# The sample rows' back products of a scan group join the insert of the last chunk's output

## The chip, the cores and the metric

The kernel runs on one core of one Trainium2 chip. The metric is the device time of one execution in microseconds. Before the change the median of three runs was 1186.1 us (1184.93 to 1188.74).

The core has five engines that run their own instruction queues in order and wait for each other by semaphores: TensorE (PE in the profile, with its weight loads as PEld), VectorE (DVE), ScalarE (ACT), GpSimd (POOL) and SyncE (SP), which here only issues DMA transfers.

## The reference, cut to what matters

One layer of a decoder: a wide input projection feeds a Mamba-2 scan (SSD) and an RG-LRU branch; both are projected, gated, merged and normed, and a gated ConvFFN follows. 512 prompt rows and 32 sample rows (8 sequences of 4 tokens, each with a state of its own) go through it together. The change touches the scan alone, which is computed for four groups of eight heads:

```python
    cb = jnp.einsum('bclgn,bcsgn->bclsg', Cm, Bm)
    y_diag = jnp.einsum('bclsg,bclsgh,bcsghp->bclghp', cb, decay, xdt)
    decay_to_end = jnp.exp(a_cs[:, :, -1:] - a_cs)
    states = jnp.einsum('bclgn,bclgh,bclghp->bcghpn', Bm, decay_to_end, xdt)
...
    y_off = jnp.einsum('bclgn,bcghpn,bclgh->bclghp', Cm, h_prev, jnp.exp(a_cs))
    y = (y_diag + y_off).reshape(b, L, SSD_HEADS, P)
...
    y = y + d_skip[:, None] * xs
    y = y.reshape(b, L, D_SSD) * jax.nn.silu(z)
```

The prompt is four chunks of 128 tokens; a sample sequence is one chunk of four tokens that starts from its stored state.

## The kernel before

**Slots.** Activations lie with channels on partitions and the 544 rows along the free axis. Every weight block of 128 output channels is one slot of the list `order`. A slot runs two half slots, 256 and then 288 columns, of 24 matmuls each (`mm3`, line 194: eight steps of the contraction, three products for a split of both operands into two fp32r parts); the weights are split into `wh` and `wl` (lines 199 and 200) two slots ahead and loaded four slots ahead into three buffers. Behind every half slot the kernel calls `hook()`.

**Inserts.** What isn't a weight slot is put between half slots. `spread(fn, slots)` fills the deque `side` with tasks and `set_rate` divides their number by the hooks of the slots (less one); each `hook()` adds this rate to a sum and runs a task for every whole number reached. So the number of tasks sets where each of them falls. The scan of group 0 is spread over ten slots (20 hooks, `p0`), those of groups 1 and 2 over fourteen (28 hooks, with the finished group's gates ahead of them), that of group 3 over twelve (24 hooks).

**A group's tasks.** `mixed_tasks(g)` (line 660) makes them of four prompt units a, b, c, d (`unit`) and one sample unit (`sample_unit`). For a prompt chunk: `s0` loads rows into E (line 441; two buffers for four chunks) and `eb`, `ep` masks E on POOL (L453) and takes exponentials on ScalarE (L456), `s1` transposes on TensorE (L465 to L467), `e1` and `e2` make `xdt` (L472, VectorE), `xde` (L474, POOL) and E times the products (L481), `st` makes the state product (L485), `pd` the products with E (L494), `py` the products with the carried state (L507), `up`, `yd` and `yo` bring these together (L511 on POOL; L513, L514, L501, L520 on VectorE).

For the sample rows, `s2(q)` for q = 0 to 3 (the tasks q0 to q3) treats two sequences each: a state product (L606), the old state times its decay on POOL (L607), and their sum on VectorE (L608), which a store then writes out. q0 and q2 also take the products of four old states with C (L600), and q2 those within the chunk (L631, TensorE) and makes from both the tile y (`joined`: L637, then four L640, all VectorE). The last task, `s4` (called f), multiplies y back into channel layout: four products (L646; eight passes in the profile, since fp32 takes two) and four VectorE operations that update the sample columns of x (L649). f needs y complete.

**Order.** Tasks put instructions into the program in this order; the library's scheduler then orders each engine's queue, and may bring instructions ahead of others that have to wait by its reckoning. Thus the next group's `s0` and `ep` (E loads on SP, L453 on POOL, L456 on ScalarE) stand ahead of much of a group's last tasks. SP issues all loads and stores, and waits in its queue wherever a buffer isn't free.

Of the kernel before, what the change touches and what calls it, by code (L numbers as in the profile page):

```python
# [78 lines left out]
def kernel(ctx: ExitStack, tc: tile.TileContext, xT, W, wdt, wab, par, con, tri,  # L79
# [574 lines left out]
    def both(*fns):  # L654
        def run():
            for f in fns:
                f()
        return run

    def mixed_tasks(g):  # L660

        a, b, c, d = (unit(g, i) for i in range(NCH))
        p0, p1, pe, q0, q1, q2, q3, f = sample_unit(g)

        def steps(*names):
            return both(*[u[n] for u, n in names])

        def first(u, v):
            return steps((u, "s1"), (v, "s1"), (u, "e1"), (v, "e1"), (u, "e2"), (v, "e2"))
        return [both(a["s0"], b["s0"], p0), steps((a, "ep"), (b, "ep")), both(p1, first(a, b)), pe,  # L670
                steps((a, "st"), (b, "st"), (a, "pd"), (b, "pd"), (a, "yd"), (b, "yd"), (c, "s0"), (d, "s0")),
                both(b["py"], q0, b["up"], b["yo"]), both(q1, c["ep"]), d["ep"], first(c, d), lambda: None,
                steps((c, "st"), (d, "st"), (c, "py"), (c, "pd"), (d, "pd"), (c, "up"), (c, "yd"), (d, "yd"), (c, "yo")),
                q2, both(d["py"], q3, d["up"], d["yo"]), f]


    yh, yl = {}, {}
# [586 lines left out]
    def p0():  # L1264
        xbc_cb(1)
        xbc_xs(1)
        zs(0)
    spread(lambda: mixed_tasks(0), p0)

    def p12(g):  # L1270
# [6 lines left out]
    def gated(g):  # L1277
        t = mixed_tasks(g)
        gt = gate_tasks(g - 1)
        return ([both(*gt[:2]), both(*gt[2:], t[0])] if g < 3 else [both(*gt), t[0]]) + t[1:]  # L1280
# [270 lines left out]
```

## Time and profile before

| | |
|---|---|
| median of three runs | 1186.1 us |
| profiled execution | 1185.91 us |
| its span | 1183.6 us |
| PE busy | 1171.3 us, 99% of the span |
| DVE, ACT, POOL busy | 751.9, 550.3 and 248.5 us |
| mean granted TensorE clock | 0.996 |
| weight matmuls' share of the chain that ended last (L194) | 88% |
| scan of the four groups | between about 65 and 434 us |

The busy time of an engine is the sum of its instructions' time without overlaps. The chain that ended last is followed back from the last instruction to what released each step; where one engine never waits, it is that engine's own instructions in order. In the rows of the chain and of the timeline the first column is the start from the beginning of the span, the second the duration; both are in us, and a number behind x counts instructions. "[0.87 <-ACT w L696]" means that the engine sat idle for 0.87 us before it, and what ended this.

### The profile page before, as it was taken

The page shows a single profiled execution, that of the slowest core. Times are in us where ns is not written, and L with a number is a line of the kernel's source. Part 1 is how long each engine was busy: PE and PEld are TensorE (multiplying, and loading weights), DVE is VectorE, ACT ScalarE, POOL GpSimd, SP SyncE. Part 2 cuts the span into 40 slices and gives each one's busy share as a digit, 9 for nine tenths or more (in the row PEclk, how much of TensorE's full clock was granted, in tenths as well). Part 3 has the DMA queues.
Part 4 walks back from the last instruction along what each step waited for, and adds up shares of the span by engine and source line. Part 5 has one row for each costly group of instructions (what it writes and reads, how often), then busy time and mean ns, then how long its engine had stood idle before and what let it go on. Part 6 is the DMA issues. An engine that isn't in the chain of part 4 may idle for free.

```text
span 1183.6 us, 22963 instructions
## 1 busy us (share of the span) xinstructions
PE 1171.3 (99%) x9390; PEld 1142.3 (97%) x9390; DVE 751.9 (64%) x1244; ACT 550.3 (46%) x1048; POOL 248.5 (21%) x341
## 2 busy tenths in 40 slices
PE   9999999999999999999999999999999999999997
PEld 7998999999999999999999999999999999999996
DVE  6888767786798777956733448774434444344456
ACT  6573654454454437568332326654313342134423
POOL 1453434343342322100100015100000010001023
PEclk9999999999999999999999999999999999999998
DMA  7436525434452621332322454442222232222312
GB/s 261 133 118 208 173 84 187 145 116 153 155 170 85 196 99 58 109 103 66 102 86 89 127 163 129 125 140 90 90 90 90 90 89 90 87 84 86 94 53 76
DMA packets 53465, 138.70 MB, mean 117 GB/s; under 512 B 5872, under 2 KB 16240, under 8 KB 53360
## 3 DMA queue, kind: packets, MB, share of 16 engines
q1 hardware_dynamic: 53360, 137.24, 36.4%
q8 instruction: 73, 1.20, 0.4%
q14 instruction: 32, 0.26, 0.1%
HBM read 124.72 MB, written 12.50 MB: 116 GB/s over the span
## 4 chain that ended last, share of the span: by engine, by line
PE 96%; DMA 1%; DVE 1%; POOL 1%; SPq 0%; issue 0%; ACT 0%; ACTq 0%; POOLq 0%
PE ps L194 88%; PE ps L494 1%; PE ps L485 1%; PE ps L507 1%; PE ps L606 1%; DMA x<-xT 1%; PE ps L600 1%; PE ps L465 1%; DMA E<-scr_a 0%; DMA wr<-W 0%; PE ps L646 0%; PE ps L467 0%; PE ps L937 0%; PE ps L944 0%; POOL h L607 0%
## 5 line engine op out<-in xcount | busy, mean ns | idle before, releaser
L194 PE MATMUL ps<-n,wh 128*128 128x256 f32 (+1 forms) x5472 | 1034.0, 288 | 1.2 <-ACT wh L199 0.8
L194 PEld LDWEIGHTS ps<-n,wh 128*128 128x128 f32 x5472 | 858.9, 188 | 7.1 <-ACT wh L199 2.0
L194 PE MATMUL ps<-n,wl 128*128 128x256 f32 (+1 forms) x2736 | 786.8, 288 | 0.1
L194 PEld LDWEIGHTS ps<-n,wl 128*128 128x128 f32 x2736 | 514.8, 188 | 0.3 <-DVE wl L200 0.3
L200 DVE TENSOR_TENSOR wl<-wr,wh 128x1024 fp32r<-128x1024 f32 (+1 forms) x183 | 226.1, 1235 | 193.1 <-ACT wh L199 192.7
L199 ACT ACTIVATE wh<-wr 128x1024 fp32r<-128x1024 f32 (+1 forms) x183 | 191.9, 1049 | 333.5 <-PE ps L194 295.6
L358 POOL COPY cffn_t<-w 128x18 f32<-128x18 f32 x24 | 18.8, 783 | 344.4 <-ACT w L1032 344.4
L362 DVE SCALAR_TENSOR_TENSOR w<-w,half_t,w 128x568 f32<-128x568 f32 x72 | 61.9, 863 | 2.4 <-ACT w L360 1.4
L362 DVE SCALAR_TENSOR_TENSOR w<-w,par_t,w 128x560 f32<-128x560 f32 (+1 forms) x72 | 59.3, 823 | 4.0 <-ACT w L360 1.0
L456 ACT ACTIVATE E<-E,nac_t 128x128 f32<-128x128 f32 x128 | 39.2, 390 | 7.1 <-POOL E L453 7.1
L199 ACT ACTIVATE n<-n 128x544 fp32r<-128x544 f32 (+2 forms) x56 | 32.2, 584 | 17.5 <-DVE n L833 10.7
L1064 DVE TENSOR_TENSOR n<-n,ps 128x256 f32<-128x256 f32 (+1 forms) x40 | 17.5, 438 | 34.6 <-PE ps L194 20.6
L607 POOL TENSOR_TENSOR h<-h,cds_t 128x512 f32<-128x512 f32 x32 | 35.7, 1147 | 6.1 <-PE ps L600 6.0
L713 POOL TENSOR_TENSOR ss<-ss,x 128x544 f32<-128x544 f32 x15 | 25.4, 1691 | 49.9 <-ACT x L712 49.4
L200 DVE TENSOR_TENSOR n<-n,n 128x544 fp32r<-128x544 f32 (+2 forms) x56 | 35.6, 641 | 0.3
L1039 ACT ACTIVATE n<-w 128x512 f32<-128x512 f32 (+1 forms) x48 | 18.2, 424 | 35.7 <-DVE w L362 35.7
L407 ACT ACTIVATE w<-w 128x568 f32<-128x568 f32 x24 | 16.3, 678 | 35.8 <-DVE w L362 35.8
L1098 DVE TENSOR_TENSOR n<-n,ps 128x256 f32<-128x256 f32 (+1 forms) x24 | 10.4, 432 | 35.5 <-PE ps L194 35.4
L1030 ACT ACTIVATE w<-ps 128x256 f32<-128x256 f32 x48 | 18.0, 375 | 31.0 <-PE ps L194 31.0
L474 POOL TENSOR_TENSOR xde<-xdt,dte_t 128x512 f32<-128x512 f32 x16 | 22.4, 1412 | 45.6 <-DVE xdt L472 45.6
L194 PE MATMUL ps<-n,n 128*128 128x256 f32 (+1 forms) x240 | 31.1, 290 | 0.0
L194 PEld LDWEIGHTS ps<-n,n 128*128 128x128 f32 x240 | 30.4, 188 | 0.1
(239 smaller groups left out, 1035.5 us busy)
## 6 DMA issues: line engine op xcount, KB each, us to landing
wr<-W SPq DMA_DIRECT2D x184, 512.0 KB, 3.5
E<-scr_a SPq DMA_DIRECT2D x16, 512.0 KB, 5.1
h<-h0T SPq DMA_DIRECT2D x32, 256.0 KB, 5.0
o_sst<-h SPq DMA_DIRECT2D x32, 256.0 KB, 2.3
eb<-scr_e SPq DMA_DIRECT2D x24, 128.0 KB, 4.8
n<-xT SPq DMA_DIRECT2D x8, 272.0 KB, 3.9
yT<-w SPq DMA_DIRECT2D x4, 288.0 KB, 2.3
x<-xT SPq DMA_DIRECT2D x4, 272.0 KB, 4.8
```

The source lines that it names most:

```text
L194: T.matmul(pt[:, :c1 - c0], a[j], b[k][:, c0:c1], start=start and i == 0 and q == 0, stop=stop and i == n - 1 and q == 2)
L199: keep(S.activation(out_h, src, AF.Copy))
L200: keep(eng.tensor_tensor(out_l, src, out_h.bitcast(F32), op=ALU.subtract))
L358: GP.tensor_copy(stage, raw[:, SEQ: SEQ + 9 * blk].rearrange("p (b s) -> p b s", s=blk)[:, :, 0:hl])
L362: V.scalar_tensor_tensor(v[:, :n], raw[:, k:k + n], wcol[:, k:k + 1], v[:, :n], op0=ALU.mult, op1=ALU.add)
L456: S.activation(E[:, h, :], E[:, h, :], AF.Exp, bias=nac_t[:, c, 8 * g + h: 8 * g + h + 1])
L474: GP.tensor_tensor(v3(xde), v3(xdt), bc_h(dte_t[:, c, hs]), op=ALU.mult)
L607: GP.tensor_tensor(v3(h0), v3(h0), bc_h(cds_t[:, b, hs]), op=ALU.mult)
L713: GP.tensor_tensor(ss, ss, y, op=ALU.add)
L1030: S.activation(raw[:, hl + c0: hl + c0 + 256], pt[:, :256], AF.Copy)
L1039: S.activation(a, b, AF.Gelu_apprx_tanh)
L1064: V.tensor_tensor(gel[m][:, a0:a1], gel[m][:, a0:a1], p_[:, :a1 - a0], op=ALU.mult)
```

## The change

The last two entries of the list of tasks become one, in which f comes first. A group has 13 tasks where it had 14:

```diff
-                q2, both(d["py"], q3, d["up"], d["yo"]), f]
+                q2, both(f, d["py"], q3, d["up"], d["yo"])]
```

With fewer tasks the rate falls, and so the places of nearly all tasks move. The hooks at which some of them fall:

| task | group 0, before / after | groups 1 and 2 | group 3 |
|---|---|---|---|
| first products of c, d (s1, e1, e2) | 13 / 14 | 18 / 20 | 16 / 17 |
| st, py, pd of c, d | 15 / 17 | 22 / 24 | 19 / 20 |
| q2 | 17 / 18 | 24 / 26 | 20 / 22 |
| py, up, yo of d with q3 | 18 / 19 | 26 / 27 | 22 / 23 |
| f | 19 / 19 | 27 / 27 | 23 / 23 |

The first place is TensorE's queue at the end of group 0, from q2's state products (L606) on; a line of "..." stands for 24 weight matmuls (L194), one half slot. Before:

```order
L606 MATMUL ps_1601<-xk_1025,bm_1247 128x512
L606 MATMUL ps_1605<-xk_1025,bm_1247 128x512
...
L507 MATMUL ps_1643<-n_332,hst_1072 128x128 x4
L606 MATMUL ps_1648<-xk_1025,bm_1247 128x512
L606 MATMUL ps_1652<-xk_1025,bm_1247 128x512
...
L646 MATMUL ps_1697<-con_t,y_1609 128x32 x4
```

And now:

```order
L606 MATMUL ps_1629<-xk_1025,bm_1292 128x512
L606 MATMUL ps_1633<-xk_1025,bm_1292 128x512
...
L646 MATMUL ps_1678<-con_t,y_1637 128x32
L507 MATMUL ps_1687<-n_332,hst_1105 128x128 x3
L646 MATMUL ps_1678<-con_t,y_1637 128x32 x3
L507 MATMUL ps_1687<-n_332,hst_1105 128x128
L606 MATMUL ps_1692<-xk_1025,bm_1292 128x512
L606 MATMUL ps_1696<-xk_1025,bm_1292 128x512
```

The back products stand one half slot behind q2 and ahead of chunk d's products, where they were two half slots and an insert behind. In groups 1 to 3 they were three half slots behind q2 (in group 3 with twelve gate matmuls between as well); there, too, it is one now.

The second place is VectorE's queue beside it, from the weight split ahead of q2's part on. Before:

```order
L200 TENSOR_TENSOR wl_1554<-wr_1359,wh_1553 128x1024
L697 SCALAR_TENSOR_TENSOR n_1457<-w_1550,ps_1525 128x288
L697 SCALAR_TENSOR_TENSOR n_1559<-w_1585,ps_1560 128x256
L637 TENSOR_TENSOR y_1609<-ps_1189,ea_t 128x512
L608 TENSOR_TENSOR h_188_1297<-h_188_1297,ps_1601 128x512
L608 TENSOR_TENSOR h_189_1299<-h_189_1299,ps_1605 128x512
L640 TENSOR_TENSOR y_1609<-y_1609,ps_1592 32x2x64 x4
```

And now:

```order
L200 TENSOR_TENSOR wl_1644<-wr_1455,wh_1643 128x1024
L697 SCALAR_TENSOR_TENSOR n_1520<-w_1613,ps_1588 128x288
L608 TENSOR_TENSOR h_185_1276<-h_185_1276,ps_1629 128x512
L608 TENSOR_TENSOR h_186_1278<-h_186_1278,ps_1633 128x512
L637 TENSOR_TENSOR y_1637<-ps_1189,ea_t 128x512
L548 TENSOR_TENSOR cmk_1928<-n_839,con_t 128x256
L640 TENSOR_TENSOR y_1637<-y_1637,ps_1620 32x2x64 x4
```

Both state updates (L608) and a mask of the next group's C (L548) now stand ahead of the part of y that they stood behind or beside. POOL's queue keeps its order there, with the masks of the next group's E ahead of the states' decay; this is the queue after the change:

```order
L511 TENSOR_TENSOR hst_1105<-hst_1105,cd_t 128x512
L453 AFFINE_SELECT E_1905<-E_1905 128x1024
L453 AFFINE_SELECT E_1907<-E_1907 128x1024
L607 TENSOR_TENSOR h_185_1276<-h_185_1276,cds_t 128x512
L607 TENSOR_TENSOR h_186_1278<-h_186_1278,cds_t 128x512
```

What moved is its place against TensorE: q2 now comes one half slot behind the products of c and d, whose end frees the E buffers.

## The prediction

> **What bounds the kernel.** I read the page first, then what TensorE waited for, then the chain of work around the ends of the four groups. The first two rows below are of the page, the others the whole list of TensorE's waits: who waited on whom, us in total, times, longest.
>
> ```profile
> span 1183.6 us, 22963 instructions
> PE 1171.3 (99%) x9390; PEld 1142.3 (97%) x9390; DVE 751.9 (64%) x1244; ACT 550.3 (46%) x1048; POOL 248.5 (21%) x341
> PE ps L1391 <- DVE w L1387: 1.5, 1, 1.5
> PE ps L944 <- DVE sd L1195: 1.0, 1, 1.0
> PE ps L194 <- ACT wh L199: 0.8, 1, 0.8
> PE ps L485 <- POOL xde L474: 0.8, 1, 0.8
> PE ps L194 <- DVE n L200: 0.4, 1, 0.4
> ```
>
> TensorE is busy for 99% of the span and waits 4.5 us in all (the rest of its idle 12.3 us lies almost wholly behind its last matmul). Only one of these waits lies in the scan (L485, in group 0); the others belong to the start and the end. So all that the other engines do is hidden, and a change of order is worth exactly the TensorE stalls that it removes or makes. The span plus 2.3 us outside it is the profiled execution's 1185.9 us, which stands 0.2 us below the median of 1186.1; I count from 1185.9. A measurement of this kernel can tell about 0.3%, 3.6 us, from no change.
>
> **What the change keeps.** The same matmuls, vector operations and transfers are issued, so the sum of work changes by nothing. What the L646 insert costs TensorE is 0.81 us a group (its row stands in the next fence), and these passes still have to run. If merging the inserts hid all of that, 4 x 0.81 = 3.2 us would go; the nearest row says that the passes take their time wherever they stand, so I take 0 and keep 3.2 as the far end.
>
> **What it removes.** A group now has 13 tasks for the same hooks, so each starts a little later after the one before. In group 0 the first products of chunks c and d and their state products were two half slots apart and are now three. The chain of waits of group 0 (start, us, what):
>
> ```profile
> 106.25 2.12 PE ps L485 x4
> 108.37 0.89 PE ps L507 x8
> 109.26 1.90 PE ps L494 x32
> 111.16 6.22 PE ps L194 x48
> 117.38 0.99 PE ps L600 x8
> 118.38 0.36 PE ps L631 x16
> 118.73 0.67 PE ps L606 x2
> ...
> 123.93 2.83 PE ps L194 x24
> 126.76 0.81 PE ps L646 x8
> ```
>
> The same place in group 1, without a wait:
>
> ```profile
> 207.72 1.72 PE ps L485 x4
> ```
>
> L485 waited 0.8 us for POOL's xde, and the second chunk's xde held it for a further 2.12 - 1.72 = 0.4. With 2.8 us more of weight matmuls ahead (a half slot, 123.93), both go: **-1.2 us**; what is late next there has over a microsecond of room.
>
> **What it adds.** The back products (L646) read y, which VectorE makes behind sample insert q2: L637, then L640, with the state updates L608 between or ahead of them. Before, L646 came two inserts and at least two half slots behind q2. Now it is the first thing in the next insert, one half slot (24 weight matmuls) behind q2, in all four groups, and q3's and chunk d's products stand behind it in TensorE's queue. So TensorE waits wherever y takes longer than one half slot.
>
> *Group 0.* POOL's and VectorE's rows here (start, us, engine, line):
>
> ```profile
> 117.15 1.09 POOL L453 TENSOR_SCALAR_AFFINE_SELECT E<-E 128x1024 f32<-128x1024 f32 x1 [5.77 <-DVE n L697]
> 118.41 1.09 POOL L453 TENSOR_SCALAR_AFFINE_SELECT E<-E 128x1024 f32<-128x1024 f32 x1 [0.17 <-PE ps L600]
> 119.47 4.05 POOL L607 TENSOR_TENSOR h<-h,cds_t 128x512 f32<-128x512 f32 x4
> 120.78 0.68 DVE L637 TENSOR_TENSOR y<-ps,ea_t 128x512 f32<-128x512 f32 x1
> 121.38 1.27 DVE L608 TENSOR_TENSOR h<-h,ps 128x512 f32<-128x512 f32 x2
> 122.57 1.19 DVE L640 TENSOR_TENSOR y<-y,ps 32x128 f32<-32x128 f32 x4
> 123.79 0.47 DVE L548 TENSOR_TENSOR cmk<-n,con_t 128x256 f32<-128x256 f32 x1
> ```
>
> POOL masks the next group's two E tiles (L453) ahead of q2's L607, and each E load waits until the last pd products (L494) have read its buffer. Before, q2 came two half slots behind L494 and POOL was nearly through; now in this group q2 comes one half slot behind. VectorE's new order puts both L608, which wait for L607, ahead of L637, L548 and L640. How long after the end of L494 the second L453 starts, in groups 1 and 2 (TensorE's L494 or what follows it, then POOL):
>
> ```profile
> 210.33 1.90 PE ps L494 x32
> 217.56 1.09 POOL L453 TENSOR_SCALAR_AFFINE_SELECT E<-E 128x1024 f32<-128x1024 f32 x1 [0.48 <-DMA E<-scr_a]
> 316.09 6.20 PE ps L194 x48
> 322.23 1.09 POOL L453 TENSOR_SCALAR_AFFINE_SELECT E<-E 128x1024 f32<-128x1024 f32 x1 [0.16 <-PE ps L194]
> ```
>
> That is 217.56 - 212.23 = 5.33 us, 322.23 - 316.09 = 6.14, and in group 0 118.41 - 111.16 = 7.25. I take the middle one. Count from the start of L494. TensorE: 1.90, half of 6.22 = 3.11, 0.99 + 0.36 + 0.67, then 2.83: it stands at L646 at 9.86. POOL: 1.90 + 6.14 = 8.04, mask 1.06 (118.41 to 119.47), two L607 of 1.01 each: 11.1. VectorE: the second L608 0.64, L637 0.60, L548 0.40, L640 1.19: y at 13.96. **+4.1 us**, with the other two delays 3.3 and 5.2.
>
> *Groups 1 and 2.* Here the distance from L494 to q2 stays two half slots, and VectorE, POOL and ScalarE keep their order between them, so y comes when it came before. VectorE's rows beside the chain's piece behind q2's L606 (48 matmuls, of which 24 now stand ahead of L646):
>
> ```profile
> 220.44 6.00 PE ps L194 x48
> 221.13 0.45 DVE L697 SCALAR_TENSOR_TENSOR n<-w,ps 128x288 f32<-128x288 f32 x1 [0.87 <-ACT w L696]
> 222.70 1.17 DVE L640 TENSOR_TENSOR y<-y,ps 32x128 f32<-32x128 f32 x4
> 324.31 6.00 PE ps L194 x48
> 327.69 1.17 DVE L640 TENSOR_TENSOR y<-y,ps 32x128 f32<-32x128 f32 x4
> ```
>
> Group 1: y at 223.87, TensorE at 220.44 + 2.83 = 223.27: **+0.6**. Group 2: 328.86 against 327.14: **+1.7**. The two differ by how long L697 waits for ScalarE, which is behind nine exponentials of the next group's E. Each could come out as the other; at the least 0.2 (group 1 with that 0.87 us wait halved) and 0.6, at the most 1.7 for both.
>
> *Group 3.* Now q2 stands behind the gate matmuls of L778, with L780 ahead of L608 on VectorE:
>
> ```profile
> 420.91 7.52 PE ps L194 x60
> 428.08 1.62 ACT L778 ACTIVATE n<-ps,bh_t 128x256 f32<-128x256 f32 x4
> 430.02 1.08 DVE L780 SCALAR_TENSOR_TENSOR n<-n,w 128x512 f32<-128x512 f32 x2
> 419.95 5.07 POOL L607 TENSOR_TENSOR h<-h,cds_t 128x512 f32<-128x512 f32 x4 [5.19 <-PE ps L600]
> ```
>
> From the end of the half slot ahead: 12 gate matmuls 7.52 - 6.00 = 1.52, L600 to L606 2.02, half slot 2.83: TensorE at 6.37. L600 ends at 2.5; two L607 at 5.07/4 = 1.27 each end at 5.05; second L608 5.7, L640 1.19: y at 6.9. **+0.5**; 0.3 with L607 at group 0's pace, 1.2 if L780 waits for ScalarE's four L778 behind a weight split.
>
> Sum: -1.2 + 4.1 + 0.6 + 1.7 + 0.5 = **+5.7 us**, 1191.6. Its own bounds: 3.3 + 0.2 + 0.6 + 0.3 - 1.2 = +3.2 (1189.1), and 5.2 + 1.7 + 1.7 + 1.2 with no gain at L485 = +9.8 (1195.7).
>
> **The rivals.** *The clock falls in group 0's stall.* A window at the end of the span (us, TensorE busy, clock) and the first matmuls of the program:
>
> ```profile
> 1175.00:1176.00 1.00, 0.89 (x6) 0.56 0.00 0
> 1.45 3.41 PE L1391 MATMUL ps<-w 128*128 128x512 f32 x4 [1.45 <-DVE w L1387]
> ```
>
> After a sparse stretch of a few us the clock is granted at half. The first four passes, out of idle, took 3.41 us, where L485's four of the same size take 1.72. So a stall of 4 us can be followed by some 3.4 us at half speed: 1.7 us more, 1193.3. Against it: 4.1 us is short. [...] Chance 0.14.
>
> *The stalls are small.* Group 0's E rows land as early as group 1's, and ScalarE delays groups 1 and 2 as little as it did group 1 at best: all terms at their low ends, +3.2, 1189.1, within 0.3%. For it speaks that 5.33 was seen; against it, that all four must be low together: group 0 at 3.3 with group 2 at 1.7 already makes +4.3 and slower. Chance 0.13.
>
> *Not slower: y is in time.* The place is q2 of group 0: if the second L453 began by 1.90 + 2.04 = 3.9 us, y would stand at 9.86 and this stall would vanish. That needs E rows about 2 us after L494, and the earliest start seen is 5.33 behind it. Were groups 1 to 3 in time too, -1.2 would remain (1184.7), and with all of the L646 inserts hidden 1181.5. Chance 0.05, of which 0.02 below -0.3%.
>
> *More falls behind.* VectorE has the sample rows' update (L649) ahead of chunk d's in the merged insert, so the gates of the finished group start later; if the next output products wait for them once, 2 us or more come on top: 1194 and up. Against it: at least three half slots lie between. Chance 0.06.
>
> **How the numbers follow.** The forecast has 0.62. With it and the cases above it 0.82 lies above 1189.7, less a little of the forecast's own low end: slower 0.79, same 0.19, faster 0.02. The range runs from just below the small stalls' 1189.1 to above the forecast's 1195.7 with part of the clock's price: 1188.0 to 1196.5.
>
> **What would show it.** TensorE's list of waits should have four new rows L646 <- DVE y L640, that of group 0 near 4 us and the others 0.5 to 2, and the L485 row should be gone. POOL's L607 in group 0 should start straight behind L453, and L608 wait for it. Wrong would be: no L646 waits; a half-speed clock in the slice near 120 us; or waits of L194 on wl or n further on.

## The result, and the profile after

| | before | after |
|---|---|---|
| median, us (lowest to highest, runs) | 1186.41 (1184.93 to 1188.74, 4) | 1197.95 (1196.28 to 1199.1, 4) |
| ratio, 95% interval | 1 | 1.0099 [1.0085, 1.0112] |
| profiled execution, us | 1185.91 | 1196.28 |
| its span, us, and granted clock | 1183.6, 0.996 | 1194.4, 0.993 |

The kernel became 11.5 us slower, 1.0%; forecast were 5.7 us, and the time lies above the range. Disturbed executions are left out of all comparisons (two of four of the kernel g123_only below, among them its profiled one, which is why it ran once more for a trace).

Two rows of the page of the kernel after, and then rows of its list of TensorE's waits (who on whom, us in total, times, longest; rows at "..." stood in the list before too):

```profile
span 1194.4 us, 22977 instructions
PE 1176.3 (98%) x9390; PEld 1145.8 (96%) x9390; DVE 757.6 (63%) x1244; ACT 548.6 (46%) x1048; POOL 242.5 (20%) x341
```
```profile
PE ps L646 <- DVE y L640: 6.3, 6, 3.3
...
PE ps L194 <- DVE n L765: 0.5, 1, 0.5
PE ps L194 <- DVE wl L200: 0.2, 1, 0.2
PE ps L606 <- DVE h L608: 0.2, 1, 0.2
...
```

The wait of L485 for xde is gone, and L646 waits 6.3 us for y. But TensorE's busy time grew too, by 5.0 us with the same 9390 matmuls: some of them ran slower. Group 0, first TensorE from L485 on, with the end of the half slot behind q2 (124.22), then POOL and VectorE (start, us, what):

```profile
111.61 1.88 PE L485 MATMUL ps<-xde,bt 128*128 128x512 f32 x4
...
114.31 1.97 PE L494 MATMUL ps<-E,xdt 128*64 128x128 f32 x32
...
124.22 0.28 PE L194 MATMUL ps<-n,wl 128*128 128x256 f32 x1
127.78 0.61 PE L646 MATMUL ps<-con_t,y 128*128 128x32 f32 x2 [3.29 <-DVE y L640]
128.21 1.63 PE L507 MATMUL ps<-n,hst 128*128 128x128 f32 x6
129.63 1.33 PE L646 MATMUL ps<-con_t,y 128*128 128x32 f32 x6
...
132.91 0.68 PE L194 MATMUL ps<-n,wh 128*128 128x288 f32 x2
...
134.21 0.43 PE L194 MATMUL ps<-n,wh 128*128 128x288 f32 x2
```
```profile
119.74 3.12 POOL L453 TENSOR_SCALAR_AFFINE_SELECT E<-E 128x1024 f32<-128x1024 f32 x2 [4.23 <-PE ps L194]
122.83 4.04 POOL L607 TENSOR_TENSOR h<-h,cds_t 128x512 f32<-128x512 f32 x4
123.90 0.69 DVE L608 TENSOR_TENSOR h<-h,ps 128x512 f32<-128x512 f32 x1 [1.63 <-POOL h L607]
124.90 0.69 DVE L608 TENSOR_TENSOR h<-h,ps 128x512 f32<-128x512 f32 x1 [0.32 <-POOL h L607]
125.51 0.68 DVE L637 TENSOR_TENSOR y<-ps,ea_t 128x512 f32<-128x512 f32 x1
126.11 1.04 DVE L548 TENSOR_TENSOR cmk<-n,con_t 128x256 f32<-128x256 f32 x1
127.08 1.19 DVE L640 TENSOR_TENSOR y<-y,ps 32x128 f32<-32x128 f32 x4
```

POOL's masks, its L607 straight behind them, both L608, then y (L637, L548, L640): the order that the prediction gave. Behind the stall the same pair of weight matmuls takes 0.68 us, and 0.43 from 134.2 on. The clock in windows of 3.41 us (the numbers behind the stretch: its length, then busy us of PE, PEld, DVE, ACT, POOL; the third from the end is the granted clock):

```profile
123.79:127.21 3.42, 0.70 (x6) 0.50 (x5) 2.99 (x5) 2.24 (x8) 3.42 (x5) 1.00 0.46 159
127.21:130.62 3.41, 2.83 (x14) 2.87 (x14) 1.74 (x6) 1.55 (x8) 1.04 (x5) 0.50 0.51 153
130.62:134.03 3.41, 3.41 (x14) 3.22 (x14) 2.69 (x8) 0.25 (x2) 1.32 (x3) 0.50 0.31 90
134.03:137.44 3.41, 3.41 (x29) 3.41 (x28) 1.84 (x4) 1.09 (x2) 0.00 (x0) 1.00 0.98 338
```

The granted clock stood at 0.50 for 6.8 us (127.21 to 134.03). By my estimate that can have cost half of it, 3.4 us, at the most, and 3.1 without the 0.6 us of it in which TensorE still waited. Groups 1 to 3 have a shorter stall each and no half speed in this trace:

```profile
235.87 0.41 PE L646 MATMUL ps<-con_t,y 128*128 128x32 f32 x2 [1.03 <-DVE y L640]
341.40 0.41 PE L646 MATMUL ps<-con_t,y 128*128 128x32 f32 x2 [1.02 <-DVE y L640]
441.31 0.41 PE L646 MATMUL ps<-con_t,y 128*128 128x32 f32 x2 [0.57 <-DVE y L640]
```

To place the loss I take from each trace the start of the first L558 of a group (TensorE, in task p1) and, as the end of group 3, of the first L849. The time from one to the next, us (from starts read to 0.1 us, so a difference of 0.1 says nothing); behind a "/" half of the time at half speed in it, the most that this can have cost:

| kernel | group 0 | group 1 | group 2 | group 3 |
|---|---|---|---|---|
| before | 90.3 | 103.8 | 102.2 | 120.8 |
| after | 96.3 / 3.4 | 105.6 | 103.9 | 122.4 |
| after, second trace | 97.5 / 3.4 | 105.3 | 105.1 / 1.7 | 122.5 |
| after, third trace | 98.0 / 3.4 | 105.3 | 102.5 | 122.4 |
| g0_only | 97.8 / 5.1 | 103.9 | 102.2 | 120.8 |
| g123_again | 90.2 | 105.7 | 102.8 | 122.4 |
| fill9 | 96.1 / 1.7 | 104.9 | 105.2 / 1.7 | 122.7 |
| fill_all | 94.8 | 104.8 | 103.5 | 123.1 |
| y_early | 91.3 | 104.5 | 102.1 | 121.5 |
| f_behind | 94.7 / 1.7 | 103.9 | 103.9 | 121.6 |
| f_behind_y | 89.5 | 103.9 | 103.5 | 121.6 |
| fourteen | 92.1 | 103.9 | 102.2 | 120.8 |

From L849 on all of them run alike (678.0 to 678.2 us from there to the first L1149, before 678.1): the whole loss lies in the four groups.

### The profile page after: what moved, and what is told of

Read it like the earlier page. It is cut to its first block, busy times and chain, and to the rows that moved or that the text cites. A ratio compares the mean times of both kernels' runs of the same rounds, so it can differ in the third digit from the quotient of the medians.

```text
span 1194.4 us, 22977 instructions
## 1 busy us (share of the span) xinstructions
PE 1176.3 (98%) x9390; PEld 1145.8 (96%) x9390; DVE 757.6 (63%) x1244; ACT 548.6 (46%) x1048; POOL 242.5 (20%) x341
## 4 chain that ended last, share of the span: by engine, by line
PE 94%; DVE 2%; DMA 1%; ACT 1%; POOL 1%; issue 0%; SPq 0%; ACTq 0%; DVEq 0%; POOLq 0%
PE ps L194 87%; PE ps L485 1%; PE ps L494 1%; PE ps L507 1%; DMA E<-scr_a 1%; PE ps L465 1%; DVE h L608 1%; PE ps L606 1%; PE ps L600 0%; PE ps L646 0%; ACT E L456 0%; DMA wr<-W 0%; PE ps L467 0%; DVE wl L200 0%; POOL xde L568 0%
## 5 line engine op out<-in xcount | busy, mean ns | idle before, releaser
L194 PE MATMUL ps<-n,wh 128*128 128x256 f32 (+1 forms) x5472 | 1034.3, 288 | 0.4 <-ACT wh L199 0.2
L194 PEld LDWEIGHTS ps<-n,wh 128*128 128x128 f32 x5472 | 859.4, 188 | 6.6 <-issue 1.8
L194 PE MATMUL ps<-n,wl 128*128 128x256 f32 (+1 forms) x2736 | 787.1, 288 | 0.3 <-DVE wl L200 0.2
L194 PEld LDWEIGHTS ps<-n,wl 128*128 128x128 f32 x2736 | 515.1, 188 | 0.7 <-DVE wl L200 0.7
L362 DVE SCALAR_TENSOR_TENSOR w<-w,half_t,w 128x568 f32<-128x568 f32 x72 | 66.1, 922 | 6.8 <-ACT w L360 5.4
L456 ACT ACTIVATE E<-E,nac_t 128x128 f32<-128x128 f32 x128 | 39.2, 390 | 10.5 <-POOL E L453 10.5
L607 POOL TENSOR_TENSOR h<-h,cds_t 128x512 f32<-128x512 f32 x32 | 38.6, 1236 | 10.0 <-PE ps L600 10.0
L194 PE MATMUL ps<-n,n 128*128 128x256 f32 (+1 forms) x240 | 31.1, 290 | 0.0
L194 PEld LDWEIGHTS ps<-n,n 128*128 128x128 f32 x240 | 30.4, 188 | 0.1
```

Source lines behind the costliest of these rows:

```text
L194: T.matmul(pt[:, :c1 - c0], a[j], b[k][:, c0:c1], start=start and i == 0 and q == 0, stop=stop and i == n - 1 and q == 2)
L362: V.scalar_tensor_tensor(v[:, :n], raw[:, k:k + n], wcol[:, k:k + 1], v[:, :n], op0=ALU.mult, op1=ALU.add)
L456: S.activation(E[:, h, :], E[:, h, :], AF.Exp, bias=nac_t[:, c, 8 * g + h: 8 * g + h + 1])
L607: GP.tensor_tensor(v3(h0), v3(h0), bc_h(cds_t[:, b, hs]), op=ALU.mult)
```

## The experiments

The theory behind them (A): TensorE's stalls for y lower the clock, and that is the half of the loss that the forecast lacks. Its rivals: half speed is no matter of the stalls or costs nothing (B); the shift of all inserts costs evenly over the four groups (C); the passes of L646 with chunk d's products in one insert are what costs, not the wait for y (D).

**Nine passes into the stall of group 0** (fill9), results overwritten by L646:

```diff
-            pt = bank()
+            pt = bank(); [T.matmul(pt, L["bm"][:, 0, :], L["xk"], start=True, stop=True) for _ in range(9 if g == 0 else 0)]
```

> The changed kernel, with nine passes of 128x512 (the form of L606, into the bank that L646 then writes over) ahead of L646 in group 0 alone, where TensorE idles 3.29 us for y. Nine such passes take some 9 x 0.36 = 3.2 us, so they add nothing to the time at which y is there. Theory A (the stall's idle is what drops the clock, and the half-speed stretch of 6.4 us behind it costs 3.2 us): no half-speed window between 127 and 135 us, span 3.2 us under the changed kernel's 1194.4, so about 1191.2, median about 1194.5. Rival B (the clock windows follow from something else in the merged insert, or cost nothing because the work behind it waits anyway): span stays within 1 us of 1194.4.

Measured: median 1197.96 us, ratio to before 1.01 [1.0079, 1.0121]: no gain, as B had it. But the trace shows that it wasn't the test it was meant to be (TensorE's rows of group 0, then windows of 3.41 us as above):

```profile
125.22 2.25 PE L644 MATMUL ps<-xk,bm 128*128 128x512 f32 x9
128.76 0.41 PE L646 MATMUL ps<-con_t,y 128*128 128x32 f32 x2 [1.28 <-DVE y L640]
```
```profile
127.54:130.96 3.42, 1.99 (x16) 1.88 (x17) 3.16 (x11) 0.83 (x4) 1.77 (x6) 1.00 0.74 226
130.96:134.37 3.41, 3.41 (x15) 3.22 (x14) 3.04 (x6) 0.98 (x5) 1.32 (x3) 0.50 0.62 205
339.17:342.58 3.41, 2.27 (x18) 1.96 (x17) 3.29 (x8) 1.56 (x6) 2.01 (x6) 1.00 0.57 186
342.58:345.99 3.41, 3.41 (x15) 3.22 (x14) 3.01 (x9) 0.42 (x1) 1.32 (x3) 0.50 0.70 197
```

The passes took 0.25 us each, so 1.28 us of idle were left, and the clock still fell, for one window in place of two. And it fell in group 2, whose code is that of the kernel after and whose idle was 0.93 + 0.22 us, where the kernel after had idled 1.02 + 0.21 us and kept the clock. So in group 2 the shorter idle lost the clock and the longer kept it, and where it falls differs between these two traces. This became theory A2, an estimate of mine from the rows above: half speed comes in stretches of some 3.4 us, and follows one in which TensorE has thin work (busy for 1.99 and 2.27 us here). That the stretches are fixed in time was part of that estimate; these rows show the length of two.

**The merged insert in one part of the groups** (g0_only; g123_only is the same with `g > 0`):

```diff
-                q2, both(f, d["py"], q3, d["up"], d["yo"])]
+                q2] + ([both(f, d["py"], q3, d["up"], d["yo"])] if g == 0 else [both(d["py"], q3, d["up"], d["yo"]), f])
```

> The merged insert in group 0 alone; groups 1 to 3 keep the 14 tasks of before. Theory A: group 0 holds -1.2 (L485) + 3.3 (idle) + 3.2 (clock) and some 0.5 of restart, together +6: span about 1189.6, median about 1192.4, one L646 wait near 3.3 us and about 6 us of half-speed clock behind it. Rival C (the loss is spread evenly over the four groups, since the shift of all inserts by the new rate is what costs): +2.5 to 3, median about 1189.

> The merged insert in groups 1 to 3; group 0 keeps the 14 tasks of before. Theory A: group 1 1.2 us of idle, group 2 1.2, group 3 0.6 and a wait on L765 of 0.5, with a restart of some 0.3 at each: +4 to +5, span about 1188, median about 1191; no half-speed window in 220 to 450 us. The L485 wait of 0.8 us in group 0 is there as before. Rival C (even spread): +7.5 to 8, median about 1194.

> The kernel of g123_only once more, for a trace: its two undisturbed runs were 1193.0 and 1194.7, 7 us over before and not the 4 to 5 that the idle of groups 1 to 3 explains. Theory A2: one or two half-speed stretches of 3.4 us (1.7 us each) behind L646 in groups 1 to 3, idle there 1.2, 1.2 and 0.6 us, and the span longer than before by about 4.5 plus 1.7 for each such stretch. Rival C: no half-speed stretch there, and the rest lies in waits elsewhere.

Measured: g0_only 1193.08 us, 1.006 [1.0045, 1.0075]; g123_only 1.0068 [1.0048, 1.0088] from two runs (1193.0 and 1194.7). In g0_only the groups 1 to 3 take what they took before, in g123_again group 0 does (table above). So the loss sits where the merge is, and the parts add up to no less than the whole. An even spread (C) falls by g0_only, where it gave 1189; the time of g123_only by itself would fit C's 1194 better than A's 1191. In g0_only group 0 holds a stall of 4.3 us and three windows at half speed, up to 5.1 us, more than the 3.2 that A gave it. g123_again, at 1189.0 us, had no half speed in the scan, where A2 gave one or two stretches of it. It had waits of 2.1 us on y and 0.5 on L765, and in group 0 one of 0.7 on L513 in place of L485's; its four stretches are 4.0 us longer than before's, of which 1.4 stand in none of the waits on y and L765. The two earlier runs lie 4 to 6 us above it, at granted clocks of 0.995 and 0.993 against 0.997: (0.997 - 0.994) x 1190 = 3.6 us of that is clock, an estimate, since the clock is listed to three decimals.

**All four stalls filled** (fill_all): the line of fill9 with `range((14, 4, 4, 2)[g])`.

> The first filled kernel still lost the clock although its stall was down to 1.28 + 0.21 us (one stretch of 3.4 us at half behind group 0's L646, and another behind group 2's, where the changed kernel with the same 1.0 us of idle kept the clock), since its nine passes took 0.25 us each and not 0.36. Here all four stalls are filled: 14, 4, 4 and 2 passes in groups 0 to 3, some 3.5, 1.0, 1.0 and 0.5 us, no more than the waits they stand in. Theory A2 (the clock is granted by fixed stretches of about 3.4 us, and one whose TensorE work is thin, idle or with few columns, is followed by one or more at half speed, 1.7 us each, in any of the four groups and not in each run): waits on y down to about 1 us, no half-speed window before 1170 us, the lateness of y remains: 1194.4 - 3.4 = span about 1191, runs closer together, median 1192 to 1193.5, 5 us under the changed kernel's. Rival B (no link between idle and clock): 1197 to 1199 again, with half-speed windows.

Measured: 1194.52 us, 1.0075 [1.006, 1.0091]; expected were 1192 to 1193.5. No window at half speed anywhere near the stalls; what is left at the stalls is the delay, and it came out longer than in the first trace of the kernel after (in group 0, 14 passes of 3.38 us and then 0.7 us of wait). One window at half speed stands elsewhere, behind a stretch in which TensorE was never idle but ran small matmuls for most of the time (L310 to L316, 43.24 to 46.3 us in the trace of before, which kept the clock there):

```profile
42.91:46.32 3.41, 3.41 (x20) 2.47 (x19) 2.78 (x6) 2.50 (x9) 3.14 (x5) 1.00 0.51 158
46.32:49.73 3.41, 3.41 (x16) 3.41 (x16) 2.20 (x4) 1.10 (x3) 0.29 (x1) 0.50 0.54 142
```

**The time lost to the clock in all runs.** Each run lists its mean granted clock; (1 - clock) x span is what it lost (in three decimals of clock, so 1.2 us for one run), including some 4 us in the last 8 us or so of the span, which before has too:

| kernel (runs) | median, us | ratio to before | mean clock loss, us |
|---|---|---|---|
| before (11, 15, 13) | 1185.2 to 1186.1 | 1 | 4.6, 3.9, 3.6 |
| after (4) | 1197.95 | 1.0099 | 9.3 |
| fill9 (4) | 1197.96 | 1.01 | 7.8 |
| fill_all (4) | 1194.52 | 1.0075 | 3.6 |
| g0_only (4) | 1193.08 | 1.006 | 8.3 |
| g123_only (2) | 1193.85 | 1.0068 | 7.2 |
| f_behind (4) | 1191.08 | 1.0052 | 5.4 |
| y_early (8) | 1188.9 | 1.0028 | 5.0 |
| f_behind_y (11) | 1187.86 | 1.0016 | 3.9 |
| fourteen (10) | 1187.52 | 1.002 | 4.4 |

The kernel after loses 5 us more to the clock than before; fill_all, in which y is no less late but TensorE has work in the place of the wait, loses none more. That settles A against B: some 5 us of the 11.5 are clock. That fill_all gained 3.4 us and not 5 goes with its longer delay.

**y ahead of the state updates** (y_early; `joined` issues L637 and L640):

```diff
                 if q == 2:
-                    within()
+                    within(); joined()
...
-                if q == 2:
-                    joined()
```

> The changed kernel, with the sum of y (L637, L640) written ahead of the two state updates L608 of insert q2, in all groups. In group 0 VectorE then has L637, one L608, L640: y comes one L608, one L607 and L548 sooner, about 2 us, so the stall falls from 3.3 to about 1.3; in groups 1 to 3 L640 stands ahead of both L608 and the waits of 1.24, 1.23 and 0.6 should fall to 0.4 or nothing. Theory A: with 1.3 us of idle the clock stays at full (1.03 us did not drop it in group 1), so 2.0 + 3.2 + about 2.5 = 7 to 8 us less than the changed kernel: span about 1187, median about 1190. Rival D (waiting for y is not what costs; the passes of L646 with chunk d's products in one insert are): L646 waits go, the time stays above 1195.

Measured: 1188.9 us, 1.0028 [1.0014, 1.0042], 9 us less than the kernel after, and no half speed in the scan. Its waits on y:

```profile
PE ps L646 <- DVE y L640: 0.9, 2, 0.7
```

So waiting for y is the cause, and D falls: the merged insert is still there. VectorE's rows show that one L608, and with it POOL, still stood ahead of y in group 0:

```profile
124.46 0.69 DVE L608 TENSOR_TENSOR h<-h,ps 128x512 f32<-128x512 f32 x1 [1.03 <-POOL h L607]
125.07 1.18 DVE L640 TENSOR_TENSOR y<-y,ps 32x128 f32<-32x128 f32 x4
```

**f behind the other products, alone and with y early** (f_behind, f_behind_y):

```diff
-                q2, both(f, d["py"], q3, d["up"], d["yo"])]
+                q2, both(d["py"], q3, d["up"], d["yo"], f)]
```

> The same 13 tasks at the same hooks, with f behind chunk d's and q3's products instead of ahead of them: L507 x8 and L606 x2 (0.9 + 0.6 us) stand ahead of L646. If only the place of f ahead of them costs: group 0's wait for y falls from 3.3 to about 1.9, those of groups 1 to 3 to nothing; with the clock drop of one or no stretch 1.2 to 3 us above before, median 1187.5 to 1189.5. If the new rate (the shift of every other insert) costs by itself: 1192 or more, without L646 waits.

> Both: f behind chunk d's and q3's products, and y summed ahead of the state updates. y_early left 0.7 us of wait in group 0, 0.2 in group 1 and one wait of 0.8 us of L606 for L608; 1.5 us more of other work ahead of L646 hides the first two. Expected waits of L646 none, the L485 wait gone (-1.2), the L606 and L765 waits of 0.8 and 0.5 perhaps left: span 1182.5 to 1184, at most 1 us either side of before, median 1185 to 1187. If the spacing of 13 tasks costs by itself, 1189 or more.

Measured: f_behind 1191.08 us, 1.0052 [1.0038, 1.0065], above the 1187.5 to 1189.5 expected. Group 0's wait is 2.0 + 0.2 us with one window at half speed, groups 1 to 3 wait 0.2 us for y in all, and other waits came in (L606 0.8, L765 1.6 us in all). f_behind_y 1187.86 us, 1.0016 [1.0007, 1.0026], where 1185 to 1187 were expected: no wait on y, none of L485, and group 0 is 0.8 us shorter than before's. That gain is lost again in groups 2 and 3 (+1.3, +0.8), of which the waits show L765's part:

```profile
PE ps L194 <- DVE n L765: 0.9, 2, 0.6
```

The rest of it I can't place. No version here beats the kernel before.

**The merged insert at the old spacing** (fourteen):

```diff
-                q2, both(f, d["py"], q3, d["up"], d["yo"])]
+                q2, both(f, d["py"], q3, d["up"], d["yo"]), lambda: None]
```

> f merged ahead of chunk d's products as in the changed kernel, but with an empty task behind it, so that a group keeps 14 tasks and every other insert stands where it stood before: what is left is f's new place alone. Group 0: q2 stays two half slots behind L494, POOL is through with E, and y should stand some 1.5 us behind TensorE in place of 3.3; the L485 wait of 0.8 us stays. Groups 1 and 2: 0.6 to 1.7 us each as in the changed kernel; group 3, where q2 is not behind the gate matmuls, 0.3 to 1. Theory (place of f and nearness of q2 to the masks of E share group 0's stall): span without clock losses 4 to 5 us over before's, and at most one half-speed stretch (1.7 us): median 1190 to 1192. Rival (f's place makes all of it): group 0's stall stays at 3.3 and the median at 1195 or more.

Measured: 1187.52 us, 1.002 [1.0008, 1.0032], 2.5 us under the least that I expected. Its waits on y, all in group 0:

```profile
PE ps L646 <- DVE y L640: 1.3, 2, 1.1
PE ps L485 <- POOL xde L474: 0.8, 1, 0.8
```

Groups 1 to 3 take what they took before, to 0.1 us, and the clock is kept. I had overlooked that with 14 tasks the last insert of groups 1 and 2 falls on hook 26 and q2 on 24: two half slots lie between, and y is in time. So moving f ahead of chunk d's products costs little by itself. What costs is f ahead together with the lost task, which pulls q2 to one half slot ahead of the last insert in all groups, and in group 0 to one half slot behind L494. Neither does all of it alone: fourteen, with f ahead at the old distances, lost 2.0 us, f_behind, with the task lost and f behind, 5.9.

**The kernel after, twice more** (after_r2, after_r3; no edit):

> The changed kernel, unaltered, for a second trace. [...] Rival (the clock depends on the length of the idle alone): groups 1 and 2 behave as in the first trace, no half speed there.

> [...]

Measured: spans of 1196.6 and 1193.9 us. Both have two windows at half speed behind group 0's stall (3.84 and 4.16 us), and after_r2 one behind group 2, where TensorE had idled 0.78 + 0.22 us, less than in the first trace, which kept the clock:

```profile
340.55:343.97 3.42, 2.42 (x20) 2.11 (x19) 3.33 (x8) 2.05 (x8) 2.65 (x7) 1.00 0.50 165
343.97:347.38 3.41, 3.41 (x16) 3.22 (x16) 2.52 (x8) 0.42 (x1) 1.32 (x3) 0.50 0.55 158
```

That speaks against the rival by which the length of the idle alone decides. In after_r3 group 2 waited only 0.17 us and kept the clock. The span of after_r3 less 1.7 us a window is 1190.5, that of after_r2 1191.5.

## Why the prediction was wrong

- **The L485 wait** (-1.2): right. Its row of 0.8 us is gone, and in the chain of waits of the kernel after L485 takes 1.72 us from 111.77 on, where it took 2.12. In f_behind_y, without a wait on y, group 0 is 0.8 us shorter on the whole.
- **Group 0's stall** (+4.1; 3.3 to 5.2): the wait and its order are right, the size nearly so. Measured idle 3.29, 3.84 and 4.16 us in the three traces. In the first, L494 starts at 114.31 and L640 ends at 127.08 + 1.19 = 128.27, 13.96 behind it, the very number counted; but that is luck. L607 started 122.83 - 114.31 = 8.52 behind L494 and not 8.04 + 1.06 = 9.10, and L548 held VectorE for 127.08 - 126.11 = 0.97 and not 0.40: two misses of 0.6 us that cancel. In the other two traces y came 14.5 and 14.8 behind L494. In the first, TensorE stood ready at 124.50 and not 124.17, and began with y's first quarters, which makes 3.29 of the 4.1.
- **Groups 1 and 2** (+0.6, +1.7): the stretches are 1.5 to 1.8 and, without half speed, 0.3 to 1.7 us longer. The sum, 1.8 to 3.5, lies about the 2.3 forecast, but not as I had split it: group 1 lost more than its 0.6 in every trace, group 2 no more than its 1.7.
- **Group 3** (+0.5; 0.3 to 1.2): its stretch is 1.6 to 1.7 us longer, of which 0.57 is the wait on y and 0.5 a new wait of L194 on L765. That new wait is a small case of the rival "More falls behind", at another place than I looked for it.
- **The sum without the clock** (+5.7; up to 9.8): the start of L1149 came 10.5, 13.3 and 10.6 us later than before; less the half speed in the scan 7.1, 8.2 and 7.2. That is within the bounds, but the forecast was 1.4 to 2.5 too low. The lists of waits account for part: on y, L765 and L608 (L606 in group 0 waits 0.2 to 0.8 us for it, a wait that I hadn't forecast) they hold 7.0, 7.8 and 7.1 us, which with the 1.2 gained at L485 leaves 1.3 to 1.6 us that stand in no row. What these are stays open.
- **The step that failed is the clock.** It stood as a rival, "The clock falls in group 0's stall", at 1.7 us and a chance of 0.14, for "4.1 us is short". In all three traces it fell, for 6.8 us each time (in the first from 127.21 to 134.03; in the two others a pair of weight matmuls that takes 0.43 us later on still took 0.68 at 134.54 and at 135.99), and in one also behind group 2, which I hadn't considered: up to 3.4 to 5.1 us where the sum had 0. I judged by the length of the idle, and took one drop to last 3.4 us, an estimate from the program's first four passes. That 4.1 us is short was an estimate too, and no run shows a length of idle at which the clock falls: in group 2 it fell behind 0.78 + 0.22 us (after_r2) and held behind 1.02 + 0.21 (the first trace). What the trace of before showed was its end: TensorE busy for 0.69 and 0.32 us in the two us from 1173 on, then 0.89 in the next, granted 0.56, and a clock of 0.50 behind it. And in the first 3.41 us at half speed behind group 0's stall (127.21 to 130.62) TensorE was busy for 2.83, with 0.57 of the stall and with passes of L646 and L507; a second such stretch followed.

The mechanism of the forecast held: y is late, in group 0 by about the amount counted, and what follows in the queue waits with it. What it lacked is the clock's term, up to 3.4 to 5.1 us, and 1.4 to 2.5 us besides.

## What to carry to other kernels

Here, with TensorE busy for 98 to 99%, the price of a stall was its idle and, on top, up to 1.7 us (an estimate: half of the time at a granted clock of 0.50) for every 3.4 us at half speed that followed: none behind 1.02 + 0.21 us of idle (group 2 in the first trace), one such stretch behind 0.78 + 0.22 (group 2 in after_r2). Where a planner spreads tasks evenly, count what a merged task does to the distances of all the others before the place of the merged one: fourteen, with the same merge and the old distances, lost 2 us and not 11.5. And group 0's stall filled almost to its end (fill_all, 0.73 + 0.22 us left) kept the clock, where nine passes that left 1.28 us of idle did not, but the delay remained; y_early, which shortens the wait itself, gained 9 us where fill_all gained 3.4.

## What the runs showed of the hardware

Half speed in the scan came in stretches of three lengths. At a granted clock of 0.50 the rows above hold 6.8 us in the kernel after (127.21 to 134.03), and 3.4 us in fill9 (from 130.96 and from 342.58), in fill_all (from 46.32) and in group 2 of after_r2 (from 343.97). f_behind has 3.4 us of it, g0_only 10.2:

```profile
127.19:130.60 3.41, 1.79 (x13) 1.68 (x14) 3.32 (x8) 0.00 (x0) 3.25 (x9) 1.00 0.71 231
130.60:134.02 3.42, 3.42 (x16) 3.42 (x15) 2.64 (x8) 0.00 (x0) 0.00 (x0) 0.50 0.63 215
```
```profile
123.84:127.25 3.41, 0.49 (x5) 0.29 (x3) 2.19 (x4) 3.41 (x13) 3.41 (x4) 1.00 0.20 77
127.25:130.67 3.42, 2.05 (x10) 2.08 (x10) 2.54 (x7) 1.26 (x6) 1.83 (x6) 0.50 0.76 235
130.67:134.08 3.41, 3.41 (x16) 3.22 (x15) 1.91 (x6) 1.04 (x5) 1.32 (x3) 0.50 0.15 46
134.08:137.49 3.41, 3.41 (x16) 3.41 (x15) 2.62 (x5) 0.00 (x0) 0.00 (x0) 0.50 0.93 313
```

So the lengths in these traces are 3.4, 6.8 and 10.2 us. What sets them isn't shown.

The length of the idle doesn't tell the falls apart in these traces: half speed followed 0.78 + 0.22 us of idle (after_r2, group 2), and a stretch with none (fill_all, 42.91 to 46.32), and none followed 1.02 + 0.21 us (after, group 2). Nor does TensorE's busy time. In the 3.4 us ahead of a fall it was 0.49 (g0_only), 0.70 (after), 1.79 (f_behind), 1.99 and 2.27 (fill9), 2.42 (after_r2) and 3.41 (fill_all). The clock stayed at 1.00 behind these, two in the kernel after, one in fill_all and one in g123_again:

```profile
233.02:236.43 3.41, 2.23 (x18) 1.91 (x16) 2.69 (x7) 2.95 (x10) 3.31 (x8) 1.00 0.24 91
338.83:342.25 3.42, 2.18 (x18) 1.87 (x17) 2.94 (x8) 2.67 (x10) 3.04 (x7) 1.00 0.32 121
```
```profile
128.24:131.65 3.41, 2.46 (x14) 1.72 (x12) 3.32 (x9) 0.65 (x3) 2.98 (x7) 1.00 0.83 263
```
```profile
42.90:46.32 3.42, 3.42 (x22) 2.48 (x20) 2.79 (x6) 2.55 (x8) 3.31 (x5) 1.00 0.56 156
```

The busy time counts small matmuls in full: L646's eight passes of 32 columns take 0.97 us in the trace of the kernel before. That the amount of work in a stretch decides is thus an estimate of mine and not shown. Why the same kernel lost the clock in group 2 in one trace and kept it in another stays open.
